# A fused encoder block: the first modulation sums move from VectorE to TensorE, projection weights are asked for one chunk earlier, and the routing pause and the gather are re-ordered

## The chip, the cores and the metric

The kernel runs on one core of a Trainium2 chip. The metric is the device time of one execution in microseconds (us). Five engines work beside each other: TensorE (PE in the profile, its weight loads PEld), VectorE (DVE), ScalarE (ACT), GpSimd (POOL) and SyncE (SP), which here only issues the large loads.

## The reference

One layer of a streaming encoder on 256 tokens of width 2048, all in float32:

```
mod = silu(c) @ ada_w + ada_b            # shift1, scale1, gate1, shift2, scale2, gate2
h = rmsnorm(x) * norm1_g * (1 + scale1) + shift1
u, v, q, k, v_b, gates = split(h @ w_in)             # 5 x 1024 and 2 x 2048 columns
y_a = spatial_gating(gelu(u), gelu(v)) @ w_branch_a  # 8 groups, 128 x 128 block-causal
y_b = band_attention(q, k, v_b) @ w_branch_b         # 16 heads, 64-frame chunks
x += gate1 * ((sigmoid(ga) * y_a + sigmoid(gb) * y_b) @ w_out)
h = rmsnorm(x) * norm2_g * (1 + scale2) + shift2
x += gate2 * moe(h)          # top 1 of 4 groups, then top 2 of 8 SwiGLU experts of width 512
return rmsnorm(x) * final_g
```

The weights of the 32 experts alone are 32 x 12.6 MB, those of the projections and of the modulation some 200 MB more; each is read once.

## The kernel before

**Buffers and queues.** Loads of 2 MB go through a ring of four buffers, `r0` to `r3` (`raws`, all named `r` in the profile); `load` (L111) and the modulation loads (L195) are issued from SP in the order in which the scheduler put them, and each waits until the last reader of its buffer is done. For the experts the ring grows to eight (`W`, `dC`, `dD`, `E` besides). A scheduler orders each engine's instructions, except where `pin` or `keep_in_program_order` holds them.

**Start.** `x` (two tiles of 128 tokens), the small vectors and the spatial weights `ws` are loaded. `ada_block(0, 4)` makes shift1 and scale1 for the first four of 16 column tiles of h: four loads of 2 MB from `ada_w`, and for each of 16 row tiles one DVE instruction (L205, L207) that adds `ada_w[row] * silu(c)[row]` into an accumulator `f`; then eight PE transposes (L217) and two reductions over the partitions (L220), and three small operations (L223 to L225) give `sh1`, `sg1`. Meanwhile ACT sums the squares of x (L251), POOL takes the root (L244), ACT scales x (L254), PE turns it (L259, 32 transposes) and ACT copies it to `hx` (L264). The turned `ws` become `wsT` (L269, L270). Then each column tile is scaled and shifted (L230), and split into a high part `hh` (tile `dC`, L233) and a low part `hl` (tile `dD`, L234).

**Projections.** `run_steps` multiplies h by a chunk of 512 rows x 1024 columns of weights in four k-steps. A step has 12 products of 128x512 (L292 to L294: high x high, low x high, high x low for two token tiles and two column halves); ACT casts the weights' high part (L318), DVE subtracts for the low part (L319), into two alternating buffers. The five `homes` (q, k, v and the two gMLP halves) are made in four blocks of four column tiles: the first block writes its sums with ACT (L351), the others add on DVE (L353). During a block, the `ada_block` of the next one runs in pieces between the steps; during the last block and all that follows the same is done for the other four modulation vectors (L435). Then come the gates beside attention and gMLP, the branches and the output projection, whose evacuation is L894 to L896.

**Routing and gather.** The last eight row tiles of gate2's second half (`LEFT = 2` loads) are not summed by DVE but by PE: `gate_steps` yields nine pairs of products, a first pair that sums the DVE accumulator over partitions with `ones` (L987), and eight with `R.scb` (L990). `fill` runs one pair after the output projection, `gate_some(6)` six while DVE works out the routing, and `gate_some(8)` the rest. With the positions known, DVE builds the 0/1 matrix `Gm` for the two token tiles (L1125, L1126), and PE multiplies `rsb` (the norm's factor) by it (L1168, result copied to `rsp`, L1173) and gathers h for all 512 token-expert pairs in four quarters `gather(q)` (L1183, 16 products each). DVE multiplies each result by `rsp` (L1196), ACT scales and shifts it (L1198), POOL copies the expert's window (L1292, L1294). The destination of quarters 0 and 1 (`x0`, `x1`) is also the buffer that their products read, so no result of a quarter is written before its 16 products are done. After quarter 1 the first half of expert 0 is multiplied (L1279), then quarters 2 and 3 follow, then its second half.

**Experts.** For each of 32 experts six loads of 2 MB (12.6 MB) come in through the ring of eight; `first_half` (L1279) and `second` (L1361) use them.

## Time and profile before

| what | value |
|---|---|
| median of 3 runs | 1690.38 us (1688.21 to 1690.66) |
| the profiled execution | 1689.86 us |
| its span in the trace | 1688.1 us |
| TensorE granted clock, mean | 0.972 |
| PE busy | 1538.8 us (91%) |
| moved by DMA | 625.25 MB, 370 GB/s over the span |

The span is what the trace covers; 1.8 us lie around it. "Granted clock" is the share of the full 2.4 GHz that TensorE was given, so 0.50 is 1.2 GHz. A busy PE may be a PE at half clock. DVE, ACT and PE wait for each other through semaphores; the trace shows for each instruction what released it.

### The profile page before, as it was taken

Reading aid. Unit: us, or ns where it says so; the run is one execution under the profiler, and the core shown is the slowest. Engines: PE = TensorE matmul, PEld = TensorE weight load, DVE = VectorE, ACT = ScalarE, POOL = GpSimd, SP = SyncE. Lnnn points to the kernel's source line nnn. Section 1 sums busy time; section 2 is a strip of 40 time slices with the busy share of each in tenths; the row PEclk is TensorE's granted clock in tenths of the full one; section 3 lists DMA queues with packets and bytes.
Section 4 is the critical chain, followed back from the end, with each engine's and each line's share of the span. In section 5 each row is a group of like instructions: output and inputs, shape, how many; then the busy total and the mean of one; then the engine's idle time right before and its main releaser. Section 6 shows DMA issues by size and latency. Waiting matters only on the chain.

```text
span 1688.1 us, 18245 instructions
## 1 busy us (share of the span) xinstructions
PE 1538.8 (91%) x6725; PEld 856.1 (51%) x6725; DVE 942.5 (56%) x1313; ACT 483.5 (29%) x785; POOL 126.3 (7%) x377
## 2 busy tenths in 40 slices
PE   2999999999999999999998989989899898898996
PEld 1777778777887776643333323334233333332432
DVE  5789999998778888734332333323333233332334
ACT  4554345675444345341110111101111011110112
POOL 1000000000000000011100101001011010100101
PEclk8999999999999999999999999999999999999998
DMA  9989897797988786899999999999999999999996
GB/s 359 343 315 341 336 341 299 296 343 273 351 313 315 305 312 244 343 384 418 416 418 417 416 418 416 417 418 416 418 416 418 418 416 418 416 417 417 416 419 245
DMA packets 135358, 625.25 MB, mean 370 GB/s; under 512 B 5720, under 2 KB 5840, under 8 KB 101856
## 3 DMA queue, kind: packets, MB, share of 16 engines
q1 hardware_dynamic: 132832, 614.49, 91.5%
q10 hardware_dynamic: 992, 5.28, 0.8%
q0 software_dynamic: 1440, 4.27, 0.8%
q8 instruction: 55, 0.90, 0.2%
q14 instruction: 39, 0.32, 0.0%
HBM read 621.91 MB, written 2.10 MB: 370 GB/s over the span
## 4 chain that ended last, share of the span: by engine, by line
PE 51%; DMA 42%; DVE 4%; issue 2%; ACT 1%; SPq 0%; POOL 0%; POOLq 0%; DVEq 0%; ACTq 0%
DMA r<-in_w_dram 22%; PE b L1279 12%; PE b L294 11%; PE b L292 11%; PE b L293 10%; DMA dC<-in_w_dram 9%; DMA E<-in_w_dram 8%; PE b L1361 3%; DMA r<-in_ada_w_dram 2%; DVE W L319 1%; DVE f L435 1%; PE b L1393 1%; DVE f L207 0%; PE b L1183 0%; PE b L593 0%
## 5 line engine op out<-in xcount | busy, mean ns | idle before, releaser
L1279 PE MATMUL b<-r,e 128*64 128x512 f32 x1024 | 376.3, 626 | 44.2 <-DMA r<-in_w_dram 43.6
L1395 DVE TENSOR_TENSOR dB<-dB,b 128x512 f32<-128x512 f32 x248 | 153.6, 681 | 317.4 <-PE b L1393 317.4
L318 ACT CAST W<-r 128x1024 fp32r<-128x1024 f32 (+1 forms) x224 | 220.8, 987 | 328.6 <-PE b L293 294.0
L319 DVE TENSOR_TENSOR W<-r,W 128x1024 fp32r<-128x1024 f32 (+1 forms) x224 | 255.8, 1147 | 64.5 <-ACT W L318 63.2
L292 PE MATMUL b<-W,dC 128*128 128x512 f32 x704 | 284.9, 405 | 5.3 <-ACT dC L233 3.7
L293 PE MATMUL b<-W,dD 128*128 128x512 f32 x704 | 280.0, 398 | 0.0
L294 PE MATMUL b<-W,dC 128*128 128x512 f32 x704 | 267.1, 398 | 2.3 <-DVE W L319 2.1
L1385 ACT CAST f<-f 64x512 fp32r<-64x512 f32 x124 | 76.4, 616 | 576.2 <-DVE dB L1395 414.2
L1279 PEld LDWEIGHTS b<-r,e 128*64 128x64 f32 x1024 | 116.7, 144 | 215.9 <-issue 144.1
L292 PEld LDWEIGHTS b<-W,dC 128*128 128x128 f32 x704 | 132.9, 189 | 40.8 <-ACT dC L233 4.1
L294 PEld LDWEIGHTS b<-W,dC 128*128 128x128 f32 x704 | 131.5, 188 | 38.9 <-DVE W L319 8.0
L435 DVE SCALAR_TENSOR_TENSOR f<-r,sc,f 128x1024 f32<-128x1024 f32 x115 | 147.2, 1281 | 4.5 <-DMA r<-in_ada_w_dram 3.7
L293 PEld LDWEIGHTS b<-W,dD 128*128 128x128 f32 x704 | 132.7, 189 | 30.4 <-issue 0.5
L1279 PE MATMUL b<-dC,e 128*64 128x512 f32 x256 | 120.0, 624 | 19.6 <-DMA dC<-in_w_dram 19.6
L1279 PE MATMUL b<-E,e 128*64 128x512 f32 x256 | 118.2, 616 | 19.4 <-DMA E<-in_w_dram 19.4
L1279 PE MATMUL b<-dD,e 128*64 128x512 f32 x256 | 127.2, 648 | 0.0
L1352 DVE TENSOR_TENSOR f2y<-f2y,b 128x256 f32<-128x256 f32 x31 | 13.1, 421 | 198.6 <-ACT f2y L1351 198.6
L1279 PE MATMUL b<-W,e 128*64 128x512 f32 x256 | 121.8, 625 | 0.0
L1361 PE MATMUL b<-r,f2y 128*64 128x512 f32 x496 | 111.3, 595 | 0.0
L1386 DVE TENSOR_TENSOR f<-f,f 64x512 fp32r<-64x512 f32 x124 | 85.1, 686 | 26.4 <-ACT f L1385 23.5
L1294 POOL COPY e<-a 128x64 f32 x256 | 68.7, 271 | 205.0 <-PE b L1279 191.1
L207 DVE SCALAR_TENSOR_TENSOR f<-r,sc,f 128x1024 f32<-128x1024 f32 x60 | 77.0, 1283 | 1.6 <-DMA r<-in_ada_w_dram 1.0
(321 smaller groups left out, 1475.5 us busy)
## 6 DMA issues: line engine op xcount, KB each, us to landing
r<-in_w_dram SPq DMA_DIRECT2D x93, 2048.0 KB, 28.2
r<-in_w_in_dram SPq DMA_DIRECT2D x36, 2048.0 KB, 8.4
r<-in_ada_w_dram SPq DMA_DIRECT2D x32, 2048.0 KB, 8.6
W<-in_w_dram SPq DMA_DIRECT2D x23, 2048.0 KB, 28.5
dC<-in_w_dram SPq DMA_DIRECT2D x23, 2048.0 KB
dD<-in_w_dram SPq DMA_DIRECT2D x23, 2048.0 KB, 28.2
E<-in_w_dram SPq DMA_DIRECT2D x23, 2048.0 KB, 28.1
r<-in_ada_w_dram SPq DMA_DIRECT2D x32, 1024.0 KB, 10.1
```

What stands on the lines that cost most here:

```text
L207: nc.vector.scalar_tensor_tensor(out=acc, in0=rw[:, jj], scalar=sc[:, j : j + 1], in1=acc, op0=ALU.mult, op1=ALU.add,)
L292: nc.tensor.matmul(o, a, wh[:, cs], start=(k == k0), stop=False)
L293: nc.tensor.matmul(o, b, wh[:, cs], start=False, stop=False)
L294: closed[0] = nc.tensor.matmul(o, a, wl[:, cs], start=False, stop=close)
L318: nc.scalar.copy(wh, src)
L319: nc.vector.tensor_sub(wl, src, wh.bitcast(F32))
L435: nc.vector.scalar_tensor_tensor(out=acc, in0=rw[:, jj, :], scalar=sc[:, j : j + 1], in1=acc, op0=ALU.mult, op1=ALU.add,)
L1279: nc.tensor.matmul(pab[a * CH : (a + 1) * CH, :], xe[:, 8 * half + j, :], w[:, j // JQ, j % JQ, :], start=(half == 0 and j == 0), stop=(ha ...
L1361: nc.tensor.matmul(po[a * CH : (a + 1) * CH, :], act[:, j, :], w[:, j, a * 512 : (a + 1) * 512], start=(j == 0), stop=(j == 3),)
L1385: pin(nc.scalar.copy(oh[r, a, :], og[r, b, :]))
L1386: pin(nc.vector.tensor_sub(oh[o, a, :], og[r, b, :], oh[r, a, :].bitcast(F32)))
L1395: pin(nc.vector.tensor_add(xa[:, t, d0 : d0 + 512], xa[:, t, d0 : d0 + 512], pr))
```

## The change

**Start.** The small vectors are loaded from SP (three loads, ahead of all others) and POOL (one) instead of ACT, and x first from ACT. A first Silu on a dummy value comes ahead of the real one. `ada_first` makes the first block's sums on PE: silu(c) is spread over 64 columns (`scb`), and each row tile of a load becomes two products of 64x512 into one bank, 32 in all; the two halves of the result are copied to `part`, turned by small products with `pick`, and shift and scale are finished for the first column tile alone and then for the other three. `hh` is then written in one step from `hx` by ACT, and `hl` from a DVE copy of the same value. x is scaled on DVE instead of ACT; the copies of the turned x alternate between ACT and DVE. Only the first quarter of the first weights chunk is asked for ahead of the fourth modulation load, the rest behind it. `ws` is loaded and turned (`turn_ws`) in the second block.

**Projections.** With `follow`, `run_steps` asks for the next home's weights ahead of its own modulation load. `ada_of` and `hurried` leave the pace of later blocks at one step per call, as it was.

**Routing and gather.** `left` adds one more row tile to the accumulator on DVE, so that there are eight pairs instead of nine, of which `gate_some(5)` runs five in the first pause. In quarter 0 the products of the first token tile come for all four banks, then the four products of the factors, then those of the second token tile.

```
     xt = [T([P, D], f"x{t}") for t in range(NT)]
-    rows = T([P, P], "a2")
-    nc.vector.memset(rows, 0.0)
-    r0 = 0
-    for src in (
-        c[0].rearrange("(j p) -> j p", p=P),
-        norm1_g[0].rearrange("(j p) -> j p", p=P),
-        ada_b[0, 0:D].rearrange("(j p) -> j p", p=P),
-        ada_b[0, D : 2 * D].rearrange("(j p) -> j p", p=P),
-        gmlp_b_s[0],
-    ):
-        nc.scalar.dma_start(out=rows[r0 : r0 + src.shape[0], :], in_=src)
-        r0 += src.shape[0]
     for t in range(NT):
         nc.scalar.dma_start(out=xt[t], in_=x[0, t * P : (t + 1) * P, :])
-    ws = [T([P, 4, P], "a0"), T([P, 4, P], "a1")]
-    for i in range(2):
-        nc.gpsimd.dma_start(out=ws[i], in_=gmlp_w_s[0, 4 * i : 4 * i + 4].rearrange("g t s -> t g s"))
+    r0 = 0
+    for src, queue in (
+        (c[0].rearrange("(j p) -> j p", p=P), nc.sync),
+        (norm1_g[0].rearrange("(j p) -> j p", p=P), nc.sync),
+        (ada_b[0, 0 : 2 * D].rearrange("(j p) -> j p", p=P), nc.sync),
+        (gmlp_b_s[0], nc.gpsimd),
+    ):
+        small = queue.dma_start(out=rows[r0 : r0 + src.shape[0], :], in_=src)
+        if queue is nc.sync:
+            small_last = small
+        r0 += src.shape[0]
+
+    nc.scalar.activation(mhalf[:, 1:2], mhalf[:, 0:1], AF.Silu)
+    nc.vector.memset(mhalf[:, 1:2], -0.5)
...
-    def ada_block(k0, n):
+    def ada_pieces(k0, n):
 
         w = n * P
-        acc = accs.sb([P, 2, w])
-        nj = 16 // n
+        nj = 4 if n > 2 or k0 == 0 else 8
         for j0 in range(0, ND, nj):
             rw = raws.sb([P, nj, 2, w])
             for m in range(2):
@@ -198,6 +200,58 @@
                         0, j0 * P : (j0 + nj) * P, m * D + k0 * P : m * D + k0 * P + w
                     ].rearrange("(j p) n -> p j n", p=P),
                 )
+            yield j0, nj, rw
+
+    def modulation(ks, sums):
+        nc.vector.tensor_add(sh1[:, ks], sums[:, 0, :], b_shift[:, ks])
+        nc.vector.tensor_add(sg1[:, ks], sums[:, 1, :], b_scale[:, ks])
+        nc.vector.scalar_tensor_tensor(
+            out=sg1[:, ks], in0=sg1[:, ks], scalar=1.0, in1=g1c[:, ks], op0=ALU.add, op1=ALU.mult
+        )
+
+    def ada_first(n):
+
+
+        w = n * P
+        scb = T([P, ND, CH], "f4")
+        nc.vector.tensor_copy(scb, sc.unsqueeze(2).to_broadcast([P, ND, CH]))
+        pick = T([P, 2], "pick")
+        nc.vector.tensor_copy(pick[:, 0:1], ident[:, 0:1])
+        nc.vector.tensor_copy(pick[:, 1:2], ident[:, CH : CH + 1])
+        pacc = bk.ps()
+        for j0, nj, rw in ada_pieces(0, n):
+            for jj in range(nj):
+                j = j0 + jj
+                for m in range(2):
+                    nc.tensor.matmul(
+                        pacc[m * CH : (m + 1) * CH, 0:w], scb[:, j, :], rw[:, jj, m, :],
+                        start=(j == 0), stop=(j == ND - 1),
+                    )
+            yield
+        part = T([P, w], "f0")
+        nc.scalar.copy(part[:, 0:P], pacc[:, 0:P])
+        nc.vector.tensor_copy(part[:, P:w], pacc[:, P:w])
+        for k0, k1 in ((0, 1), (1, n)):
+            tp = sk.ps()
+            for i in range(k0, k1):
+                nc.tensor.matmul(
+                    tp[:, 2 * (i - k0) : 2 * (i - k0) + 2], part[:, i * P : (i + 1) * P], pick,
+                    start=True, stop=True,
+                )
+            modulation(slice(k0, k1), tp[:, 0 : 2 * (k1 - k0)].rearrange("p (a b) -> p b a", b=2))
+            for j in range(k0, k1):
+                s, b = sg1[:, j : j + 1], sh1[:, j : j + 1]
+                nc.scalar.activation(hh[:, j, :], hx[:, j, :], AF.Identity, bias=b, scale=s)
+                full = scr[:, j * S : (j + 1) * S]
+                nc.vector.tensor_scalar(full, hx[:, j, :], s, b, op0=ALU.mult, op1=ALU.add)
+                nc.vector.tensor_sub(hl[:, j, :], full, hh[:, j, :].bitcast(F32))
+        yield
+
...
+    first = ada_first(BLOCKS[0])
+    with tc.issue_after(small_last.ins):
+        next(first)
     ss1 = T([P, NT], "ss1")
     scr = T([P, D], "e2")
-    for t in range(NT):
-        nc.scalar.activation(scr, xt[t], AF.Square, accum_out=ss1[:, t : t + 1])
+    with tc.issue_after(sc_made.ins):
+        for t in range(NT):
+            nc.scalar.activation(scr, xt[t], AF.Square, accum_out=ss1[:, t : t + 1])
     rs1 = inv_rms(ss1, "n1")
     for t in range(NT):
-        nc.scalar.activation(xt[t], xt[t], AF.Copy, scale=rs1[:, t : t + 1])
+        nc.vector.tensor_scalar(xt[t], xt[t], rs1[:, t : t + 1], None, op0=ALU.mult)
+    turned = Ring(["b2", "b3", "b4", "b5", "b6", "b0"])
     for j in range(0, ND, 2):
-        tp = bk.ps()
+        tp = turned.ps()
         for jj in range(2):
             for t in range(NT):
                 nc.tensor.transpose(
@@ -261,22 +335,43 @@
                     xt[t][:, (j + jj) * P : (j + jj + 1) * P],
                     ident,
                 )
-        nc.scalar.copy(hx[:, j : j + 2, :], tp.rearrange("p (a b) -> p a b", a=2))
+        tv = tp.rearrange("p (a b) -> p a b", a=2)
+        if j % 4 == 0:
+            nc.scalar.copy(hx[:, j : j + 2, :], tv)
+        else:
+            nc.vector.tensor_copy(hx[:, j : j + 2, :], tv)
+    with tc.issue_after(small_last.ins):
+        next(first)
+        next(first)
+
+        early = [raws.sb([P, 4, CW])]
+        nc.sync.dma_start(out=early[0][:, 0, :], in_=w_in[0, 0:P, 2 * GW : 2 * GW + CW])
+        for _ in first:
+            pass
     wsT = T([P, 8, P], "f3")
-    for i in range(2):
-        tp = bk.ps()
-        for g in range(4):
-            nc.tensor.transpose(tp[:, g * P : (g + 1) * P], ws[i][:, g, :], ident)
-        nc.scalar.copy(wsT[:, 4 * i : 4 * i + 4, :], tp.rearrange("p (a b) -> p a b", a=4))
-    nc.gpsimd.memset(wsT[CH:P, :, 0:CH], 0.0)
-    for _ in first:
-        pass
-
-
...
+            src = w[q * P : (q + m) * P, c0 : c0 + cw].rearrange("(j p) n -> p j n", p=P)
+            if early:
+                rw = early.pop()
+                tc.keep_in_program_order(nc.sync.dma_start(out=rw[:, 1:m, :], in_=src[:, 1:m, :]))
+            elif fetched:
+                rw = fetched.pop()
+            else:
+                rw = load([P, m, cw], src)
+            if follow is not None:
+
+                nk, nn, nc0 = follow
+                fetched.append(
+                    load([P, nn, cw], w[nk * P : (nk + nn) * P, nc0 : nc0 + cw].rearrange("(j p) n -> p j n", p=P))
+                )
...
+            follow = None
+            if h + 1 < len(homes):
+                follow = (k0, n, homes[h + 1][0])
+            elif not lastb:
+                follow = (k0 + n, BLOCKS[b + 1], homes[0][0])
...
+        if b == 0:
+            sides.append(turn_ws())
...
+            acc = accs[len(units) - 1]
+            j = ND - 4 * LEFT
+            nc.vector.scalar_tensor_tensor(
+                out=acc, in0=fetched[-LEFT][:, 0, :], scalar=sc[:, j : j + 1], in1=acc,
+                op0=ALU.mult, op1=ALU.add,
+            )
+            return fetched[-LEFT:], acc
...
-    gate_some(6)
+    gate_some(5)
...
+    def factors():
+        for t in range(NT):
+            for i in range(2):
+                pin(
+                    nc.tensor.matmul(
+                        prs, rsb[:, i, t, :], Gm[:, t, :], start=(t == 0 and i == 0), stop=(t == 1 and i == 1)
+                    )
+                )
+        nc.vector.tensor_copy(rsp, prs)
+
     rsp = T([P, PAIRS], "f2x")
-    nc.vector.tensor_copy(rsp, prs)
     Xg = []
 
     def gather(q):
-        banks = []
-        for j in range(JQ):
-            pg = bk.ps()
+        banks = [bk.ps() for _ in range(JQ)]
+
+        def products(j, t):
+            for i in range(2):
+                pin(
+                    nc.tensor.matmul(
+                        banks[j], x1p[q, t][i][:, j, :], Gm[:, t, :],
+                        start=(t == 0 and i == 0), stop=(t == 1 and i == 1),
+                    )
+                )
+
+
+        if q == 0:
             for t in range(NT):
-                for i in range(2):
-                    pin(
-                        nc.tensor.matmul(
-                            pg, x1p[q, t][i][:, j, :], Gm[:, t, :],
-                            start=(t == 0 and i == 0), stop=(t == 1 and i == 1),
-                        )
-                    )
-            banks.append(pg)
+                for j in range(JQ):
+                    products(j, t)
+                if t == 0:
+                    factors()
+        else:
+            for j in range(JQ):
+                for t in range(NT):
+                    products(j, t)```

The instruction order on PE at the start, from the program's first product to its first projection (names are tile_number; `a` holds the small vectors, then `ws`; `x` the tokens, `f` the accumulator, `r` the loads). Before:

```order
L169 MATMUL b_10_88<-ident_64,a_7_75 128x128
L259 MATMUL b_22_109<-ident_64,x_5_73 128x128
...
L259 MATMUL b_29_151<-ident_64,x_6_74 128x128
L269 MATMUL b_31_158<-ident_64,a_8_84 128x128 x4
L269 MATMUL b_32_164<-ident_64,a_9_85 128x128 x4
L217 MATMUL b_39_201<-ident_64,f_33_171 128x128 x4
L217 MATMUL b_40_207<-ident_64,f_33_171 128x128 x4
L292 MATMUL b_49_245<-W_63,dC_97 128x512
```

And now (`f_16_96` is `scb`, `f_36_206` is `part`):

```order
L172 MATMUL b_8_85<-ident_66,a_2_64 128x128
L226 MATMUL b_18_101<-r_19_102,f_16_96 64x512 x8
L226 MATMUL b_18_101<-r_32_171,f_16_96 64x512
L333 MATMUL b_24_123<-ident_66,x_6_75 128x128
...
L333 MATMUL b_31_165<-ident_66,x_7_76 128x128
L226 MATMUL b_18_101<-r_32_171,f_16_96 64x512 x7
L226 MATMUL b_18_101<-r_33_182,f_16_96 64x512 x8
L226 MATMUL b_18_101<-r_35_195,f_16_96 64x512 x8
L237 MATMUL b_37_209<-pick_98,f_36_206 128x2
L237 MATMUL b_38_217<-pick_98,f_36_206 128x2 x3
L387 MATMUL b_48_252<-W_63,dC_94 128x512
```

The 32 transposes of x stand between the first nine and the other 23 products of the sums, and the turning of `ws` is gone from here.

The order in which SP asks for the first loads. Before:

```order
L195 DMA r_34_172<-in_ada_w_dram 128x4x512 x2
L195 DMA r_35_179<-in_ada_w_dram 128x4x512 x2
L195 DMA r_36_186<-in_ada_w_dram 128x4x512 x2
L195 DMA r_37_193<-in_ada_w_dram 128x4x512 x2
L111 DMA r_46_233<-in_w_in_dram 128x4x1024
```

And now:

```order
L164 DMA a_2_64<-in_c_dram 16x128
L164 DMA a_2_64<-in_norm_g_dram 16x128
L164 DMA a_2_64<-in_ada_b_dram 32x128
L197 DMA r_19_102<-in_ada_w_dram 128x4x512 x2
L197 DMA r_32_171<-in_ada_w_dram 128x4x512 x2
L197 DMA r_33_182<-in_ada_w_dram 128x4x512 x2
L348 DMA r_34_193<-in_w_in_dram 128x1024
L197 DMA r_35_195<-in_ada_w_dram 128x4x512 x2
L405 DMA r_34_193<-in_w_in_dram 128x3x1024
```

The fourth modulation load now goes into the buffer of the first (`r0`) and stands behind a quarter of the weights.

PE from the routing pause to the end of quarter 0. Before (`f_442` is the DVE accumulator, `E` the routing's small tiles, `f_470` is `Gm`, `f2y_4712` is `rsb`, `x_430` quarter 0's tokens, `x_434` quarter 1's):

```order
L990 MATMUL b_457_4651<-r_454_4531,E_3826 64x512 x8
L990 MATMUL b_457_4651<-r_456_4649,E_3826 64x512 x4
L1101 MATMUL b_468_4739<-E_3826,ones_69 128x96 x2
...
L990 MATMUL b_457_4651<-r_456_4649,E_3826 64x512 x4
L1168 MATMUL b_476_4782<-f_470_4755,f2y_4712 128x512 x4
L1183 MATMUL b_480_4801<-f_470_4755,x_430_4298 128x512 x4
...
L1183 MATMUL b_485_4831<-f_470_4755,x_434_4317 128x512 x4
```

And now (`f_472` is `Gm`, `x_432` quarter 0's tokens):

```order
L1111 MATMUL b_459_4674<-r_456_4553,E_3848 64x512 x6
L1111 MATMUL b_459_4674<-r_458_4671,E_3848 64x512 x4
L1222 MATMUL b_470_4760<-E_3848,ones_71 128x96 x2
...
L1111 MATMUL b_459_4674<-r_458_4671,E_3848 64x512 x4
L1306 MATMUL b_482_4817<-f_472_4776,x_432_4320 128x512 x2
...
L1291 MATMUL b_478_4803<-f_472_4776,f2y_4733 128x512 x4
L1306 MATMUL b_482_4817<-f_472_4776,x_432_4320 128x512 x2
...
L1306 MATMUL b_487_4852<-f_472_4776,x_436_4339 128x512 x4
```

Ten products stand in the pause instead of twelve, and eight gather products stand ahead of the factors' four.

## Rows read from the trace of the kernel before

**Rows 1.** The page: GB/s of DMA in 40 equal slices of the span.

```profile
GB/s 359 343 315 341 336 341 299 296 343 273 351 313 315 305 312 244 343 384 418 416 418 417 416 418 416 417 418 416 418 416 418 418 416 418 416 417 417 416 419 245
```

**Rows 2.** Busy time by stretch: stretch, length, PE, PEld, DVE, ACT, POOL, clock, DMA share, GB/s.

```profile
45.00:100.00 55.00, 54.70 (x227) 43.30 (x228) 43.12 (x44) 30.29 (x44) 0.00 (x0) 0.95 0.93 350
...
160.00:220.00 60.00, 58.83 (x256) 46.80 (x255) 57.78 (x69) 26.26 (x33) 3.48 (x5) 1.00 0.85 318
...
640.00:700.00 60.00, 56.58 (x252) 40.60 (x251) 48.73 (x65) 31.28 (x55) 0.00 (x0) 1.00 0.67 250
...
836.00:1616.00 780.00, 697.56 (x2934) 267.18 (x2934) 261.34 (x442) 100.64 (x208) 76.64 (x259) 0.96 1.02 417
```

**Rows 3.** The chain in 0 to 60 us: start, length, work.

```profile
18.29 14.49 DMA r<-in_ada_w_dram
...
43.23 0.17 DVE sg L225
...
43.48 1.09 ACT dB L230 x2
...
44.92 0.80 PE b L292
...
49.59 0.43 PE b L293
...
52.16 0.23 PE b L294
```

**Rows 4.** The timeline, 0 to 30 us: start, length, instruction [idle before, releaser].

```profile
15.21 1.91 ACT L251 ACTIVATE e<-x 128x2048 f32<-128x2048 f32 x1 [3.56 <-DMA x<-in_x_dram]
16.66 0.76 DVE L205 TENSOR_SCALAR f<-r,sc 128x1024 f32<-128x1024 f32 x1 [6.53 <-DMA r<-in_ada_w_dram]
...
18.90 1.75 POOL L244 TENSOR_TENSOR rs_n<-ve_n,mhalf 128x2 f32<-128x2 f32 x1 [13.22 <-DVE ve_n L242]
20.68 3.90 ACT L254 ACTIVATE x<-x,rs_n 128x2048 f32<-128x2048 f32 x2 [3.47 <-POOL rs_n L244]
...
22.73 5.53 PE L259 MATMUL b<-ident,x 128*128 128x128 f32 x32 [12.93 <-ACT x L254]
...
28.10 1.04 PE L269 MATMUL b<-ident,a 128*128 128x128 f32 x8
```

**Rows 5.** Busy time by stretch (columns of rows 2): DMA rate, and the clock's fall.

```profile
20.00:30.00 10.00, 6.26 (x40) 5.62 (x40) 8.95 (x8) 8.28 (x11) 0.64 (x1) 1.00 1.05 386
...
32.00:33.00 1.00, 0.00 (x0) 0.00 (x0) 0.84 (x2) 0.00 (x0) 0.00 (x0) 0.95 1.05 412
33.00:34.00 1.00, 0.00 (x0) 0.00 (x0) 1.00 (x1) 0.00 (x0) 0.00 (x0) 0.50 1.02 406
```

**Rows 6.** Waits of PE between 50 and 700 us: total, times, longest.

```profile
PE b L294 <- DVE W L319: 4.3, 6, 1.7
PE b L292 <- ACT W L318: 1.6, 3, 1.1
```

**Rows 7.** The timeline of the routing pause and the gather.

```profile
703.29 5.37 PE L990 MATMUL b<-r,E 128*64 128x512 f32 x24
...
707.57 0.22 DVE L1093 TENSOR_TENSOR E<-E 128x64 f32<-128x64 f32 x1
...
708.59 0.69 PE L1101 MATMUL b<-E,ones 128*128 128x96 f32 x4
...
712.29 0.71 PE L1168 MATMUL b<-f,f2y 128*128 128x512 f32 x2 [0.53 <-DVE f L1126]
...
713.60 0.70 PE L1168 MATMUL b<-f,f2y 128*128 128x512 f32 x2 [0.60 <-DVE offc L1132]
...
714.14 7.63 PE L1183 MATMUL b<-f,x 128*128 128x512 f32 x32
```

**Rows 8.** SP's issues at the end of the gather.

```profile
744.32 0.55 SPq L111 DMA_DIRECT2D W<-in_w_dram  x1
```

**Rows 9.** Busy time (columns of rows 2) around that issue.

```profile
742.00:747.00 5.00, 3.66 (x22) 1.67 (x18) 0.00 (x0) 2.52 (x5) 3.42 (x18) 1.00 0.39 121
```

More of the change, by code (lines that the diff above doesn't have):

```diff
@@ L139, in flush @@
             tick()
+    rows = T([P, P], "a2")
+    nc.vector.memset(rows, 0.0)
     ident = T([P, P], "ident")
@@ L200, in ada_block @@
                 )
+            yield j0, nj, rw
[40 more added lines that the diff above has]
+        yield
+    def ada_block(k0, n):
+        w = n * P
+        acc = accs.sb([P, 2, w])
+        for j0, nj, rw in ada_pieces(k0, n):
             yield
@@ L222, in ada_block @@
             )
-        nc.vector.tensor_add(sh1[:, ks], sums[:, 0, :], b_shift[:, ks])
-        nc.vector.tensor_add(sg1[:, ks], sums[:, 1, :], b_scale[:, ks])
-        nc.vector.scalar_tensor_tensor(
-            out=sg1[:, ks], in0=sg1[:, ks], scalar=1.0, in1=g1c[:, ks], op0=ALU.add, op1=ALU.mult
-        )
+        modulation(ks, sums)
         yield
@@ L234, in ada_block, with ada_of, hurried @@
             nc.vector.tensor_sub(hl[:, j, :], hx[:, j, :], hh[:, j, :].bitcast(F32))
-            if j % 2 == 1:
+            if (j - k0) % 2 == 1 or j == k0 + n - 1:
                 yield
+    def ada_of(k0, n, calls):
+        parts = [n] if n <= 4 else [3, n - 3]
+        blocks, steps = [], 0
+        for m in parts:
+            blocks.append(ada_block(k0, m))
+            steps += (4 if m > 2 else 2) + ND + 1 + (m + 1) // 2
+            k0 += m
+        return hurried(itertools.chain(*blocks), max(1.0, steps / calls))
+    def hurried(g, rate):
+        due = 0.0
+        while True:
+            due += rate
+            while due >= 1.0:
+                due -= 1.0
+                if next(g, "end") == "end":
+                    return
+            yield
     def inv_rms(ss, name):
@@ L263, in hybrid_block, with turn_ws, run_steps @@
                 )
[L264 to L276 removed]
+        tv = tp.rearrange("p (a b) -> p a b", a=2)
[10 more added lines that the diff above has]
+            pass
+    wsT = T([P, 8, P], "f3")
+    def turn_ws():
+        ws = [T([P, 4, P], "a0"), T([P, 4, P], "a1")]
+        with tc.issue_after(casts[-1].ins):
+            for i in range(2):
+                nc.scalar.dma_start(out=ws[i], in_=gmlp_w_s[0, 4 * i : 4 * i + 4].rearrange("g t s -> t g s"))
+        yield
+        for i in range(2):
+            tp = sk.ps()
+            for g in range(4):
+                nc.tensor.transpose(tp[:, g * P : (g + 1) * P], ws[i][:, g, :], ident)
+            nc.scalar.copy(wsT[:, 4 * i : 4 * i + 4, :], tp.rearrange("p (a b) -> p a b", a=4))
+            yield
+        nc.gpsimd.memset(wsT[CH:P, :, 0:CH], 0.0)
+        yield
+    def run_steps(lh, ll, w, k0, n, c0, evac, with_ada=None, cw=CW, after=None, follow=None):
         nhf = cw // 512
         npc = 4096 // cw
+        npc = -(-n // -(-n // npc))
         pt = []
```

30 lines of the change are left out of this document (12 added, 18 removed).

## The prediction

> **What bounds the kernel now.** I read the page first: the GB/s row, which lies near 417 from the 19th slice to the last but one and lower and uneven before it [rows 1]. Then busy time by stretch, which says what each half waits for. From 836 to 1616 us the loads run at 417 GB/s without a break while PE is busy 697.6 of 780 us: the experts are bound by DMA [rows 2]. From 45 to 700 us it is PE: it idles 0.3 us in 45 to 100, 1.17 in 160 to 220, 3.42 in 640 to 700 [rows 2]. So the kernel is a stretch paced by PE, then a stream of bytes whose rate nothing here changes. A load is issued when a reader frees its buffer, so the stream starts when PE gets there. A microsecond saved on PE's way to 700 us is a microsecond at the end, as long as DVE and the loads keep pace with PE; one saved between 700 and 744 us counts only while DMA stands idle. The chain of waits then shows the way to the first projection: the modulation loads, DVE's sums, transposes, a first product at 44.92 us [rows 3]. The timeline of that stretch gives what the pieces cost [rows 4], a finer table by stretch the clock [rows 5], and the timelines of the gather and of SP the second place [rows 7, 8].
>
> **The start.** The last of the four modulation loads lands at 32.78 us (18.29 + 14.49) [rows 3]; then come four DVE sums, eight transposes, reductions, modulation, scaling and split, and PE starts at 44.92, 12.1 us after the landing. It starts at half clock: products follow each other every 0.43 us, and later every 0.23 [rows 3]. The clock had dropped to 0.50 in the 33rd microsecond, when PE had been idle since the end of the transposes at 29.14 (28.10 + 1.04) [rows 4, 5]. With 12 products of 0.427 us the first k-step ends at 50.05.
>
> Now the same with the change. *Landing.* Ahead of the fourth load's end stand x (2.1 MB), four loads (8.4) and a quarter of the weights (0.5); before it was `ws` (0.5) in the place of that quarter. The bytes are equal, and DMA was busy throughout at 386 GB/s [rows 5]. I take 32.0 us, a little early for the small packets of `ws` that are gone; the bounds are 31.3 and 33.5. The fourth load needs `r0`, whose products end by about 17 us, when some 3 MB still queue, so that wait is covered. *Products.* A pair of 64x512 products has a row: 24 records, that is 12 products, in 5.30 us or so, 0.44 us each [rows 7]. A load is eight of them, 3.5 us, against 5.4 us for its bytes (2.1 MB at 386 GB/s). PE must have the rest done when the last load lands. x's second half has its squares done at 17.2 us now [rows 4]; asked for first, it should land some 3 us earlier, near 12.3, so squares end near 14.4, POOL's root (1.75) near 16.6, and DVE's scaling of the two tiles, 1.5 us each (twice the 0.76 of 128x1024), at 18.2 and 19.7; ACT took until 24.6 [rows 4]. The transposes stand behind the first product of the second load, which lands near 18.5 to 19; they take 5.5 us [rows 4], to 24.6; then 15 products, 6.6 us, to 31.2. That is just before 32.0, so the last eight start on landing and end at 35.5. *Tail.* Copy to `part`, small products, three DVE operations of 0.17, one ACT instruction of 0.55 (half of 1.09) [rows 3] and the handoffs: 2.0 us is my estimate (1.5 to 3.0). First projection at 37.5, and, at full clock, 12 x 0.233 = 2.8 us later, at 40.3, the first k-step is done. DVE has the low part of the second column tile ready at about the same time, so I see no new wait there. **40.3 - 50.05 = -9.75 us.**
>
> The clock in this sum rests on a pattern: PE is never idle for over 2 us from 13 us on, and before, an idle stretch of 13 us ahead of the transposes (12.93 us, to 22.73 [rows 4]) still found the full clock. The Trainium skill (TensorE: Matmul & The Clock Gate, Part 4: PE-mode transpose) says that the full clock does not engage for transposes, since they do not count as busy in the same way. Here the 32 transposes ran in 5.53 us with the clock at 1.00 in their stretch [rows 4, 5], but nothing shows whether they hold it up. By that rule the clock could fall in the middle of the new chain; what this would cost is a rival below.
>
> **What is moved behind the start.** The eight transposes of `ws` took 1.04 us beside DVE's sums, where PE had nothing to do [rows 4]. Now they stand in the second block, where PE sets the pace: **+1.04 us.** Their load is asked for about four k-steps before PE needs it, so it is covered; the two copies are on ACT, which is busy 26 of 60 us there [rows 2].
>
> **Weights a chunk ahead.** I cost it at nothing. Each load still needs the buffer of the load four earlier in the ring, so a home's weights are asked for when those of two homes earlier have been split, as before: about 11 us before they are needed, of which the transfer takes 5.4. In the second and third block SP now often issues a modulation load ahead of weights, but its buffer is free earlier too. The possible gain is small: waits for a split are 4.3 + 1.6 us in all of 50 to 700 [rows 6].
>
> **The pause and the gather.** In the pause PE ends its twelve products only as L1101 starts at 708.59, though DVE had its operand at 707.79 (707.57 + 0.22) [rows 7]. With ten products PE is free at 707.7: the chain is 0.78 us earlier. Next, PE waits between the two pairs of factor products, from about 12.8 to 13.60, and quarter 0 is 16 products of 0.234 behind them [rows 7]. Now eight gather products fill that time, since they need only the first tile's matrix; of the 36 products from 712.29 to the end of quarter 1 at 721.77, none waits any more: 36 x 0.234 = 8.4 us instead of 9.5. In all quarter 1 ends some 1.65 to 1.85 us earlier, and with it expert 0's first half, the other quarters and the second half, at whose end SP asks for the next load, at 744.32 [rows 8]. DMA had run dry by then: in 742 to 747 us it moved 121 GB/s, so 5 x (1 - 121/417) = 3.55 us were lost [rows 9]. An issue 1.65 us earlier fills that much: **-1.65 us.** Were the stream not dry, this part would be worth nothing. The added DVE sum (1.28 us) falls into the last output chunk, where DVE, busy 48.7 of the 60 us in 640 to 700 [rows 2], has time to spare and the split is a step ahead: nothing, at most half of it, 0.6.
>
> **Sum.** -9.75 + 1.04 - 1.65 = -10.4 us against the profiled 1689.86: 1679.5. That execution lies 0.5 us below the median of 1690.38, so I predict **1680.0 us**.
>
> **Rivals.**
> *A: the clock falls among the transposes and comes back.* For it speaks the rule above. Coming back took about 5 us of dense products (44.92 to 50). Six of the 15 products then cost 0.87 instead of 0.44: the last eight start at about 33.5, end at 37: 1681.5; two such dips 1684.
> *B: half clock throughout, from the first sum to the end of the first k-step.* Loads' products take 7 us, transposes about 8.6: PE is at 29.5 after them, at 42.4 after 15 products, 49.3 after the last, 51.3 with the tail, and 56.4 after the first k-step: 6.4 us later than before, so 1690.4 + 6.4 + 1.04 - 1.65 = **1696, slower**. It decides when PE still has over some 14 us of sums left as the last load lands; against it speaks the full clock until 32.9 us [rows 5]. If only what follows the transposes stays at half, it is about 1691.
> *C: the middle eats part of it.* DVE is busy 57.8 of 60 us in 160 to 220 [rows 2]. If weights land behind a modulation load asked for at the same moment, they come 5.4 + 5.4 + 2 us after the issue, 1.4 us late; in four homes that is 5.6 us: 1685.6.
> *D: x or the small vectors come late*, so transposes start near 22 instead of 19: the sums end 2 to 3 us later, 1682.5.
> *E: weights a chunk ahead does work*, and the 5.9 us of split waits [rows 6] mostly go: 1675.
>
> **Chances.** The forecast, 1677.5 to 1682.5: 0.66. A 0.10, D 0.06, C 0.08, E 0.03, about 1691 0.03, B 0.04. The low end takes the best tail, landing and gather (-1.5 - 0.7 - 0.2, and 1 us of split waits): 1676.5; the high end reaches A, D and C: 1686.5. What a measurement of this kernel can tell from no change is about 0.2%, 3.4 us. Faster by more than that (below 1687.0): 0.88; within: 0.07; slower: 0.05.
>
> **What the profile will show.** Right: the first L387 near 37.5 us and PE's clock 1.00 from 13 us on; L226 in groups of eight of 3.5 us; stretches of 45 to 700 as full as before but some 9 us earlier; and DMA's hole before the third load of `W` down to 1.9 us. Wrong: a clock of 0.50 before 40 us; PE waiting for DVE's split in the second and third block more than 5 us; quarter 1 no earlier against the end of the output projection; or a stream of experts that does not run at 417.

## The result

The changed kernel takes **1705.45 us** (median of 4 runs, 1704.63 to 1706.60), the kernel before 1690.25: a ratio of 1.0094 (95% interval 1.0081 to 1.0106), 15.2 us slower. Forecast were 1680.0 us and a range of 1676.5 to 1686.5. The profiled execution took 1706.04, its span is 1704.2. From the first expert load into `W` to the end of the span it takes 989.2 us, where it took 990.4 before; the time is lost ahead of the experts. The start comes first. The timeline of PE in the changed kernel, 9 to 41 us (start, length, instruction, idle time before it), answers to [rows 3, 4]:

```profile
12.31 1.94 PE L226 MATMUL b<-r,f 128*64 128x512 f32 x2 [2.67 <-DMA r<-in_ada_w_dram]
14.93 5.91 PE L226 MATMUL b<-r,f 128*64 128x512 f32 x16 [0.68 <-DMA r<-in_ada_w_dram]
20.77 3.71 PE L333 MATMUL b<-ident,x 128*128 128x128 f32 x32
24.41 7.09 PE L226 MATMUL b<-r,f 128*64 128x512 f32 x32
32.46 3.65 PE L226 MATMUL b<-r,f 128*64 128x512 f32 x14 [0.96 <-DMA r<-in_ada_w_dram]
36.46 0.38 PE L237 MATMUL b<-pick,f 128*128 128x2 f32 x2 [0.36 <-ACT f L232]
37.28 0.80 PE L237 MATMUL b<-pick,f 128*128 128x2 f32 x6 [0.43 <-DVE sg L207]
38.07 0.73 PE L387 MATMUL b<-W,dC 128*128 128x512 f32 x2
39.18 0.50 PE L388 MATMUL b<-W,dD 128*128 128x512 f32 x1 [0.38 <-DVE dD L247]
...
40.82 0.63 PE L388 MATMUL b<-W,dD 128*128 128x512 f32 x1
```

The start went nearly as forecast: the last modulation load lands at 32.4, the sums end at 36.11 (32.46 + 3.65), the first projection comes at 38.07. Busy time by stretch shows the clock (the third column from the end): it is full among the transposes and is 0.50 in 40 to 43 us.

```profile
20.00:25.00 5.00, 5.00 (x40) 3.78 (x38) 2.48 (x4) 2.35 (x4) 0.00 (x0) 1.00 1.05 390
...
40.00:43.00 3.00, 3.00 (x9) 2.32 (x8) 2.43 (x5) 1.00 (x3) 0.00 (x0) 0.50 1.03 383
...
100.00:160.00 60.00, 49.59 (x209) 39.05 (x209) 47.99 (x54) 22.35 (x28) 0.52 (x1) 0.94 0.78 284
160.00:220.00 60.00, 55.27 (x238) 43.43 (x237) 55.82 (x65) 23.28 (x28) 1.53 (x2) 1.00 0.82 302
```

Where the lead goes is in the last two rows: PE has 49.59 us of work in 100 to 160 and 55.27 in 160 to 220. The kernel before had 58.83 in the second of these stretches [rows 2], and in the first:

```profile
100.00:160.00 60.00, 58.94 (x258) 46.88 (x257) 55.86 (x62) 26.77 (x34) 0.00 (x0) 1.00 0.88 327
```

The waits of PE in the changed kernel (total, times, longest), in 100 to 160 the first two, in 160 to 220 the third, in 220 to 280 the fourth:

```profile
PE b L362 <- DMA a<-in_gmlp_w_s_dram: 6.6, 1, 6.6
PE b L389 <- DVE W L427: 3.0, 3, 1.7
...
PE b L389 <- DVE W L427: 4.7, 4, 2.3
...
PE b L389 <- DVE W L427: 3.7, 2, 2.3
```

The end of each home tells it most plainly. The table takes the moment at which the first of a home's four evacuations (L351 and L353 before, L459 and L461 now) starts, and gives for each kernel how much later than before it is (minus: earlier). The columns to the right belong to the experiments below. Each column is read from one profiled execution; that of run 1 (1693.39 us) was 2.5 us slower than the median of its runs.

| home's end | before, us | changed | weights as before | and `ws` early | casts first at three ends | chunk ahead, on the kernel before |
|---|---|---|---|---|---|---|
| block 1, 1st | 56.64 | -6.95 | -7.03 | -7.00 | -6.86 | 0.37 |
| 2nd | 67.84 | -6.95 | -5.15 | -5.12 | -6.10 | 0.38 |
| 3rd | 79.05 | -6.97 | -3.27 | -3.25 | -5.61 | 0.38 |
| 4th | 90.27 | -6.51 | -1.41 | -1.39 | -5.45 | 0.35 |
| 5th | 103.61 | -6.78 | -0.67 | -0.64 | -4.72 | -0.86 |
| block 2, 1st | 114.34 | 8.08 | 2.13 | 0.23 | -3.85 | 4.15 |
| block 3, 2nd | 185.55 | 14.29 | 2.18 | 0.28 | -3.78 | 10.54 |
| block 4, 5th | 279.24 | 17.27 | 2.59 | 0.34 | -3.98 | 11.28 |

The lead of 7 us is whole until the first block's end and gone at once: 14.9 us are lost between the fifth home and the next, 9 more until the fourth block's end.

### The profile page after: what moved, and what is told of

Same layout as the page of the kernel before. It is cut to its first block, busy times and chain, and to the rows that moved or that the text cites. A ratio compares the mean times of both kernels' runs of the same rounds, so it can differ in the third digit from the quotient of the medians.

```text
span 1704.2 us, 18349 instructions
## 1 busy us (share of the span) xinstructions
PE 1559.1 (91%) x6785; PEld 865.0 (51%) x6785; DVE 930.8 (55%) x1314; ACT 477.0 (28%) x776; POOL 126.3 (7%) x376
## 4 chain that ended last, share of the span: by engine, by line
PE 44%; DMA 42%; issue 6%; DVE 5%; ACT 1%; POOL 0%; SPq 0%; POOLq 0%; DVEq 0%; ACTq 0%
DMA r<-in_w_dram 22%; PE b L1413 12%; DMA dC<-in_w_dram 9%; PE b L389 9%; PE b L387 8%; DMA E<-in_w_dram 8%; PE b L388 8%; PE b L1495 3%; DMA r<-in_ada_w_dram 2%; DVE W L427 2%; DVE f L261 1%; PE b L1527 1%; PE b L226 1%; DMA a<-in_gmlp_w_s_dram 1%; PE b L1306 0%
## 5 line engine op out<-in xcount | busy, mean ns | idle before, releaser
L427 DVE TENSOR_TENSOR W<-r,W 128x1024 fp32r<-128x1024 f32 (+1 forms) x224 | 255.1, 1144 | 81.7 <-ACT W L426 80.5
L387 PE MATMUL b<-W,dC 128*128 128x512 f32 x704 | 283.7, 404 | 3.1 <-ACT W L426 3.1
L388 PE MATMUL b<-W,dD 128*128 128x512 f32 x704 | 280.2, 398 | 0.4 <-DVE dD L247 0.4
L389 PE MATMUL b<-W,dC 128*128 128x512 f32 x704 | 267.8, 400 | 12.2 <-DVE W L427 12.1
L1413 PEld LDWEIGHTS b<-r,e 128*64 128x64 f32 x1024 | 120.3, 146 | 212.3 <-issue 139.0
L389 PEld LDWEIGHTS b<-W,dC 128*128 128x128 f32 x704 | 131.1, 188 | 50.9 <-DVE W L427 20.2
L387 PEld LDWEIGHTS b<-W,dC 128*128 128x128 f32 x704 | 132.9, 189 | 38.9 <-ACT W L426 5.5
L549 DVE SCALAR_TENSOR_TENSOR f<-r,sc,f 128x1024 f32<-128x1024 f32 x115 | 147.0, 1279 | 3.9 <-DMA r<-in_ada_w_dram 3.2
L388 PEld LDWEIGHTS b<-W,dD 128*128 128x128 f32 x704 | 132.8, 189 | 31.7 <-issue 0.8
L1413 PE MATMUL b<-E,e 128*64 128x512 f32 x256 | 124.4, 643 | 22.9 <-DMA E<-in_w_dram 22.9
L1413 PE MATMUL b<-dC,e 128*64 128x512 f32 x256 | 116.2, 608 | 17.8 <-DMA dC<-in_w_dram 17.8
L1413 PE MATMUL b<-dD,e 128*64 128x512 f32 x256 | 123.3, 630 | 0.4 <-DMA dD<-in_w_dram 0.4
L1413 PE MATMUL b<-W,e 128*64 128x512 f32 x256 | 117.4, 608 | 0.3 <-DMA W<-in_w_dram 0.3
L1413 PEld LDWEIGHTS b<-E,e 128*64 128x64 f32 x256 | 36.4, 147 | 80.8 <-issue 48.6
```

The lines of the kernel that those rows point to most:

```text
L387: nc.tensor.matmul(o, a, wh[:, cs], start=(k == k0), stop=False)
L388: nc.tensor.matmul(o, b, wh[:, cs], start=False, stop=False)
L389: closed[0] = nc.tensor.matmul(o, a, wl[:, cs], start=False, stop=close)
L427: nc.vector.tensor_sub(wl, src, wh.bitcast(F32))
L549: nc.vector.scalar_tensor_tensor(out=acc, in0=rw[:, jj, :], scalar=sc[:, j : j + 1], in1=acc, op0=ALU.mult, op1=ALU.add,)
L1413: nc.tensor.matmul(pab[a * CH : (a + 1) * CH, :], xe[:, 8 * half + j, :], w[:, j // JQ, j % JQ, :], start=(half == 0 and j == 0), stop=(ha ...
```

## The experiments

**The theories.** *Q, the queue's order:* SP asks in order. A home's weights wait for the buffer that the home before gives back; now the modulation load of a home stands behind the weights of the next one, and so behind a wait that ends about a home, 11.2 us, later. DVE's sums then end with the block and not a home ahead. *S:* the late `ws` load and what follows it start it all. *M:* the early start itself asks more of DMA and DVE than they have. What Q looks like in the changed kernel, on SP and on DVE:

```profile
59.47 0.37 SPq L111 DMA_DIRECT2D r<-in_w_in_dram  x1
60.66 1.08 SPq L197 DMA_DIRECT2D r<-in_ada_w_dram  x2
71.52 0.37 SPq L111 DMA_DIRECT2D r<-in_w_in_dram  x1
74.03 0.92 SPq L197 DMA_DIRECT2D r<-in_ada_w_dram  x2
...
95.32 3.92 DVE L261 SCALAR_TENSOR_TENSOR f<-r,sc,f 128x1024 f32<-128x1024 f32 x3
100.05 0.69 DVE L274 TENSOR_REDUCE sums<-b 128x4 f32<-128x512 f32 x1 [0.81 <-PE b L271]
```

The last modulation load for the second block goes out at 74.03; DVE ends its sums at 99.24 (95.32 + 3.92), when PE has ended the block's last product at 98.9. What SP waited for ahead of the loads at 71.52 and 74.03:

```profile
SPq L111 <- DVE W L427: 9.7, 1, 9.7
SPq L197 <- DVE f L261: 2.1, 1, 2.1
```

The weights load waits 9.7 us for a buffer, and the modulation load behind it is not issued meanwhile; then it waits 2.1 us for its own buffer.

**1. Weights as before.** `with_ada=nxt, follow=follow` becomes `with_ada=nxt`; all else as changed.

> The changed kernel, but each home's weights are asked for in their own home again (no weights load ahead of the modulation load on SP); all else stays. Theory Q (queue order: a weights load that waits for its buffer holds back the modulation load behind it by one home of about 11.2 us, so DVE's sums end at the block's end instead of a home earlier): the sums for the second block end some 10 us before the first block's end, PE is fuller in 100 to 280 us, and about two thirds of the 24.8 us that are lost between the first and the 80th weight cast come back; what stays is the wait for ws: 1686 to 1692 us. Theory S (the late ws load and the half clock behind it start it all, and DVE never catches up): 1702 to 1706 us. Theory M (the early start itself asks more of DMA and DVE in the middle than they give): 1698 us or more, with PE waiting for the splits as in the changed kernel.

Measured: 1690.87 us, ratio to before 1.0007 (0.9997 to 1.0016): 14.6 us back. The same rows of this run:

```profile
61.30 0.37 SPq L111 DMA_DIRECT2D r<-in_w_in_dram  x1
65.14 0.92 SPq L197 DMA_DIRECT2D r<-in_ada_w_dram  x2
...
87.35 3.92 DVE L261 SCALAR_TENSOR_TENSOR f<-r,sc,f 128x1024 f32<-128x1024 f32 x3
92.08 0.69 DVE L274 TENSOR_REDUCE sums<-b 128x4 f32<-128x512 f32 x1 [0.81 <-PE b L271]
```

The load goes out 8.9 us earlier and the sums end at 91.27, 11.7 us ahead of the fifth home's end (103.61 - 0.67). Q holds; S falls, and the total is not M's either (1698 or more). The Trainium skill (DMA: Bandwidth & Descriptors, Anatomy of one DMA — SWDGE (gpsimd) path) says that a transfer's wait for a semaphore happens on the sequencer that issues it, before dispatch. The rows agree (the section is on transfers that GpSimd issues, these are SP's): in the changed kernel the modulation loads at 60.66 and 74.03 are issued only once the weights' have been, at 59.47 and 71.52.

**2. `ws` asked for early.** The two loads move into a generator that runs in the first block:

```
+    def load_ws():
+        with tc.issue_after(casts[-1].ins):
+            ...
+    sides.append(load_ws())
```

> The changed kernel, but the two loads of ws are issued in the first block behind the second weight cast (about 38 us) instead of at its end (99.01 us); the eight transposes stay where they are. Theory Q: the wait of 6.6 us for ws goes, but PE then waits for the first scaled column tile until about 104.7 instead of starting it at 108.8, so 4 us come back and perhaps 1.5 of the half clock: 1699 to 1702 us. Theory S: most of the loss goes, 1682 to 1688 us. Theory M: 1699 to 1702, as Q.

Measured: 1702.01 us, ratio 1.0074 (1.0057 to 1.0091): 3.4 us back, a little less than the 4 of Q. The wait for `ws` is gone; the other cost of the late sums is not. Not all of the 3.4 us need be the load's: in the profiled execution the clock stayed full in 40 to 43 us, and the first home ended 8.58 us earlier than before instead of 6.95.

**3. Chunk ahead on the kernel before.** `follow` and `fetched` alone are added to it.

> The kernel before, with one thing of the change: each home's weights are asked for a home ahead, in front of the modulation load. Theory Q: the modulation loads go out a home later, the sums end at the block's end in every block, and this alone costs 10 to 18 us: 1700 to 1708 us. Theory S and theory M: no late ws and no early start, so within 2 us of 1690.3; what the prediction had said of this edit is the same, nothing or up to 5.9 us faster.

Measured: 1702.68 us, ratio 1.0075 (1.0058 to 1.0092): 12.5 us slower, with no early start and no late `ws`. DVE's last sum of the first block's `ada_block` ends at 99.65 in it, and PE waits for the splits in 100 to 280 us:

```profile
98.37 1.28 DVE L209 SCALAR_TENSOR_TENSOR f<-r,sc,f 128x1024 f32<-128x1024 f32 x1
...
PE b L296 <- DVE W L327: 10.1, 6, 3.7
```

**4. Modulation load ahead.** In the changed kernel two statements change places: `next(with_ada, None)` stands ahead of the load for `follow`.

> The changed kernel with two statements swapped: the modulation load of a home is issued ahead of the next home's weights load, so that weights are still asked for a home ahead but no modulation load stands behind them. Theory Q (the modulation loads lose a home on SP's queue): the sums end about a home before the first block's end again, the 24.8 us shrink as in the run with the weights as before, 1688 to 1693 us. Rival P (asking for weights ahead fills the ring of four buffers, whichever stands first, so DVE's sums and the splits stay late): 1700 us or more.

Measured: 1690.51 us, ratio 1.0001 (0.9991 to 1.0010). The two statements are all that differs from the changed kernel, and they set the order on SP: so it is the place on the queue. Rival P is not tested apart from that: in the first two blocks the loads are issued in the very order of run 1, so that on SP the weights are not ahead any more.

**5. Both: weights as before, `ws` early.**

> The changed kernel with both: weights asked for in their own home, ws loaded in the first block. Theories Q and S: the gain of the start at the first block's end (6.95 us by the casts) and that of the gather (1.2 us at the end) stay, less 1.04 us for the transposes of ws in the second block: 1682 to 1685 us. Theory M: the middle eats the start's gain, 1688 to 1691 us.

Measured: 1689.66 us, ratio 1.0002 (0.9993 to 1.0012). Against run 1 the 1.2 us for `ws` are about what its noise allows. This is a miss for Q: the lead of 7.00 us at the first home's end is 0.64 at the fifth's, some 1.9 less at each end of a home. M, or something else, was still to be found.

**6. Pause and gather alone**, on the kernel before.

> The kernel before with the last part of the change alone: the added DVE sum, eight pairs of gate products with five in the pause, and the first tokens first in the gather's first quarter. By the prediction's term 1.65 us faster, 1688.5 us; by the changed kernel's trace (late by 17.3 us at the last weight cast, 15.6 at the 11th expert load, 16.1 to 16.5 among the experts) some 1 us of it is left at the end, 1689.0 us. Rival G (the stream has no hole that could be filled once the loads behind are counted): 1690.1 us.

Measured: 1688.69 us, ratio 0.9995 (0.9985 to 1.0004). The median moves by 1.4 us; the interval takes in nothing as well. The traces agree with a gain: SP issues the load of [rows 8] at 742.81 instead of 744.32, and the expert loads behind it land 1.5 us earlier in the median.

**7. Chunk ahead in the first block alone**, `ws` early (`if b == 0 and h + 1 < len(homes)`).

> The changed kernel with ws loaded in the first block and the weights asked for a home ahead in the first block alone, not across its end nor in the others. Theory Q: inside the first block PE keeps 7 to 8 us, as in the changed kernel, and pays about 6 us at its end for the sums that come too late; the other blocks lose nothing more: 1687 to 1691 us. Rival P: the late sums of the first block carry over into the next ones, 1695 us or more. If the sums came in time, 1682 us.

Measured: 1693.26 us, ratio 1.0022 (1.0012 to 1.0031). Between the two expectations. ACT's weight casts run 8.4 us ahead of before in the first block, 1.7 behind at the second home's cast of the next one, 4.3 behind in the fourth: the late sums cost more than the lead. (The clock stayed full in 40 to 43 us here too.)

**8. Fewer bytes**, on run 5: for `k0 == 4` only `rw[:, 0]` is loaded and used.

> The version with the weights as before and ws loaded in the first block (1689.66 us), but of the modulation weights for the second block only one row tile of four is loaded and used four times, which leaves out 6.3 MB of loads during the first block; the instructions on PE, DVE and ACT are the same. Theory D (with an earlier start the first block is bound by its loads, 400 GB/s from 50 to 80 us, and so eats the start's gain): PE's waits for weights of 5.3 us between 36 and 100 us go, the weight casts stay 8 to 10 us earlier than before up to the first block's end, and the total falls to 1680 to 1684 us. Theory M2 (DVE or the order of its sums eats the gain): no more than 2 us faster than 1689.66.

Measured: 1682.14 us, ratio 0.9963 (0.9949 to 0.9977): the lead stays, 6.1 to 7.5 us at the ends of the first block's homes. It looks like proof of D, but the scheduler plans with the loads and wrote another order for ACT as well; at the second home's end a cast now stands ahead of the copies, which it does not in run 5 (below):

```profile
60.12 1.05 ACT L430 CAST W<-r 128x1024 fp32r<-128x1024 f32 x1 [1.75 <-PE b L392]
61.08 1.96 ACT L463 COPY e<-b 128x512 f32<-128x512 f32 x3
```

So the run says that the lead can be kept, not why.

**9. A spare buffer.** On run 5, the second home's weights go to the two x buffers.

> The version with the weights as before and ws loaded in the first block (1689.66 us), and the second home's weights of the first block loaded into the two x buffers, which are free from the last transpose (24.4 us) until the fourth home writes its results there; the ring of four buffers is then one load ahead in the first block. All bytes are loaded. Theory D (the first block is bound by its loads, and the hole in them at 45 to 50 us, where 214 GB/s were moved because all four buffers were taken, makes it worse): weights for the third home land near 58 us instead of 61.4, those for the fourth near 68 instead of 72.3, both before PE needs them; PE's waits for weights of 5.3 us go, and the total is 1682 to 1685 us. If the bytes alone decide, whatever the buffers: 1687 to 1690 us. Theory M2 (DVE's order): no change, 1689 to 1690 us.

Measured: 1688.72 us, ratio 0.9994 (0.9985 to 1.0003): not D's total, but that for "the bytes alone decide". DMA moved 372 GB/s in 45 to 50 us instead of 214, and nearly nothing came of it: the third home's weights landed at 60.7 us, the fourth's at 71.2. What run 5's waits of 1.6 us wait for is in its own trace. PE's waits in 36 to 100 us, and ACT at the second home's end:

```profile
PE b L390 <- ACT W L429: 5.3, 4, 1.6
...
62.72 2.68 ACT L462 COPY e<-b 128x512 f32<-128x512 f32 x4 [2.68 <-PE b L392]
65.30 2.00 ACT L429 CAST W<-r 128x1024 fp32r<-128x1024 f32 x2
```

The weights had landed at 61.4; the cast that PE waits for stands behind four copies, and these behind PE's last product of the home. In the kernel before the cast comes first at this end:

```profile
66.89 1.05 ACT L318 CAST W<-r 128x1024 fp32r<-128x1024 f32 x1 [1.75 <-PE b L293]
67.84 1.97 ACT L351 COPY e<-b 128x512 f32<-128x512 f32 x3
```

*Theory O:* the order of ACT costs 1.6 us and more at each end. That the scheduler chose it because it took the loads to come late is a guess. The Trainium skill (Perfetto Trace Analysis, Tensor Engine Instruction) says that ACT takes its instructions strictly in order; these rows agree.

**10. Casts first.** `tc.keep_in_program_order` on ACT's casts and copies of the first block, on run 5.

> The version with the weights as before and ws loaded in the first block (1689.66 us), and in the first block ACT's casts and evacuation copies held in the order of the program: a home's first cast ahead of the four copies of the home before (in 1689.66 us they stand behind them, and PE idles 1.6 us for that cast at each of four ends of homes). Theory O (this order of ACT, made for loads that come late, eats the start's gain): the four waits of 5.3 us and what follows them go, PE ends the first block 5 to 7 us earlier, total 1682 to 1686 us. Theory D (the weights themselves land too late: third home's at 61.4, fourth's at 72.3 us): the cast then stands waiting for its load, PE's waits stay within 1 us of 5.3, total 1688.5 to 1690.5 us.

Measured: 1693.76 us, ratio 1.0028 (1.0019 to 1.0037). A miss that decides nothing: the hold also put the very first cast behind the writing of `hh` (first cast at 40.6 instead of 27.0 us) and delayed the block's end. With the spare buffer besides it was 1694.38, where O had 1682 to 1686 and D about 1688.7: a miss too. **11. At the four inner ends alone:**

> The version with the weights as before and ws loaded in the first block (1689.66 us), with the hold on ACT's order at the four ends of homes inside the first block alone: the next home's first cast ahead of the four copies; the start and the block's end are left to the scheduler, since the wider hold put the first cast of all behind the writing of hh (first product 4 us later) and delayed the block's end. Theory O: first weight cast at 27 us as in 1689.66 us, no wait of 1.6 us at the ends of homes, PE ends the block 5 to 7 us earlier than with 1689.66 us, total 1682 to 1685 us. Theory D (loads): the held cast waits for its weights, which landed at 61.4 and 72.3 us; PE's waits stay near 5 us and the total within 1.5 us of 1689.66.

Measured: 1690.64 us, ratio 1.0002 (0.9993 to 1.0011). The total is the one of D, within 1.5 us of 1689.66, and a miss for O. But the lead was 6.66, 6.33 and 6.21 us at the first three ends, as O says, and then the copies of the fourth stood behind the scaling of the next block's columns. With the spare buffer it was 1692.06, where 1682 to 1685 (O) or within 1.5 of 1688.72 (D) had been expected. **12. At the first three ends alone**, where the cast and the copies change places on ACT and a product or so on PE; up to 280 us, SP and DVE keep the order of run 5:

```
-                    casts.append(nc.scalar.copy(wh, src))
+                    casts.append(hold[0](nc.scalar.copy(wh, src)) if first_cast else nc.scalar.copy(wh, src))
```

> The same hold at the first three ends of homes only, where ACT's order differs from 1689.66 us in nothing but the first cast standing ahead of the four copies. With the hold at four ends PE kept its lead (6.66 us at the first end, 6.21 at the third, against 7.00 and 3.25 without) and lost it at the fourth, where the copies came to stand behind the scaling of the next block's columns (PE waited for the banks), so the total did not move. Theory O: a lead of 6 us at the third end, one wait of 1.6 to 1.9 us at the fourth, about 4 us at the block's end and in the blocks behind, total 1685 to 1687 us. If the weights bind (third home's landed at 60.5, fourth's at 71.8 us): the lead is lost to 3 us and less by the block's end, total 1688 to 1690 us.

Measured: **1685.88 us**, ratio **0.9980 (0.9971 to 0.9990)**: 0.2% faster than the kernel before, and inside O's range. ACT at the second end, and PE's waits for the casts in 36 to 100 us:

```profile
60.78 1.05 ACT L430 CAST W<-r 128x1024 fp32r<-128x1024 f32 x1 [1.86 <-DMA r<-in_w_in_dram]
61.74 2.56 ACT L463 COPY e<-b 128x512 f32<-128x512 f32 x4
...
PE b L391 <- ACT W L430: 0.5, 1, 0.5
```

The cast now waits for its load (1.86 us) and is still in time for PE. So the order ate most of the lead, and the loads stand close behind it: the lead at the fifth home's end is 4.72 us, not 7.00. O holds. That the loads (D) are the next limit is argued from this wait; no run shows it, and what takes the other 2.3 us of the lead was not parted further.

## Why the prediction was wrong, point by point

**The step that failed** is "Weights a chunk ahead. I cost it at nothing". Its reason, that SP often issues a modulation load ahead of weights "but its buffer is free earlier too", looked at the buffers and at one direction of the exchange. What changed is that the modulation load stands behind the next home's weights, whose buffer comes free a home later. Runs 1 and 3 price it from both sides: 14.6 us with the change around it, 12.5 alone, where 0 was written and up to 5.9 faster was rival E. One of the signs of being wrong that the prediction names came with it: PE waited for DVE's split 3.0 + 4.7 = 7.7 us in the second and third block, where more than 5 was to count. Rival C had the queue's order as its mechanism, but the wrong way round (weights behind modulation) and at 5.6 us.

**The start** was to give 9.75 us. Its pieces came within 0.6 us (32.4 for 32.0; 36.1 for 35.5; 38.07 for 37.5), but the first k-step ended near 43.0, not 40.3: 7.0 us at the first home's end. Some 1.4 of these 2.7 us are the clock, 0.50 from 40 to 43 us: in runs 2 and 7, where it stayed full, the step ended at 41.6 and 41.7, and the lead at the first home's end was 8.58 and 8.43. The rest is the start of the projection, 0.6 us late, and small waits in the step, of which the profile shows one of 0.38 us for DVE's split of h. That the sum then carried this to the end of the kernel was the second fault, hidden behind the first: with the weights as before it is worn down to 0.64 at the block's end (run 5); with all loads in place and ACT's order mended, 4.72 are left there (run 12). "As long as DVE and the loads keep pace" was said and not worked out.

**The clock.** PE was to be at full clock from 13 us on; through the start it was, but for the 3 us from 40 on, which come behind a stretch (36.1 to 39.5) with three gaps of 0.36 to 0.43 us and a handful of products. These gaps alone do not explain the fall: runs 2 and 7 have them too, and run 2 shows in 40 to 43 us

```profile
40.00:43.00 3.00, 3.00 (x15) 2.40 (x14) 2.71 (x6) 1.80 (x3) 0.00 (x0) 1.00 1.03 383
```

Rival A put the fall among the transposes, by the rule of the Trainium skill (TensorE: Matmul & The Clock Gate, Part 4: PE-mode transpose); here 32 transposes ran in 3.71 us at a clock of 1.00, among products. Rival B did not come.

**`turn_ws`** was to cost 1.04 us with its load "asked for about four k-steps before PE needs it". It was issued at 99.01, at the block's end, took 8.95 us beside a modulation load issued at 95.43 and a weights load issued at 99.27, and PE waited 6.64 us. Of these at most 3.4 us mattered in the changed kernel (run 2), since the first scaled column tile was not there until about 104.7 either; 1.2 with the weights as before. The turning itself was sized about right: in runs 5 and 12 the lead shrinks by 0.87 us between the last home of the first block and the next, where the transposes stand.

**Pause and gather** held: L1222 comes at 725.23, and the 36 products from 728.81 to 737.35 take 8.5 us instead of 9.5. Counted from the output projection's end, where the kernel is 17.3 us late, L1222 comes 0.66 us earlier than L1101 did (forecast 0.78), and quarter 1 ends 1.72 us earlier (1.65 to 1.85). The rows of the changed kernel that answer to [rows 8, 9]:

```profile
759.90 0.55 SPq L111 DMA_DIRECT2D W<-in_w_dram  x1
...
757.00:762.00 5.00, 4.24 (x24) 1.83 (x20) 0.00 (x0) 1.95 (x4) 4.04 (x20) 1.00 0.80 297
```

The hole shrank from 3.55 to 1.4 us (5 x (1 - 297/417)), or to 1.6 in 757.58 to 762.58, the stretch that lies about the issue as that of [rows 9] does (283 GB/s); 1.9 was forecast. The kernel was 17.3 us late ahead of the pause (first load into `W` issued at 715.05 instead of 697.75) and 16.1 by the spans: 1.2 of the 1.65 are there at the end, 1.4 in run 6.

**The sum** by the runs: 1689.66 - 1690.13 for what is left in run 5, + 1.2 for the late `ws` (run 1), + 14.6 for the queue: 15.3. It meets the 15.2 measured by construction, since each term is the step from one run to the next, and proves nothing. What speaks for the size of the queue's term is that it comes out alike in other company: 12.5 on the kernel before (run 3), 12.35 with `ws` asked for early (1702.01 - 1689.66).

## What to carry to other kernels

A load that is asked for earlier on an in-order queue delays everything behind it until its buffer is free: price a prefetch by what stands behind it, not by its own wait. When an early stage is sped up, follow its lead from end to end of the next units before writing it down to the end of the kernel; an order of instructions that is fixed ahead of time can give it back although the data come in time. And where an experiment takes bytes away, look whether the order of the engines changed with it.

## What the runs showed of the hardware

The clock was 1.00 through the start although PE had idled 9.19 us before its first product and 2.67 after it; it fell to 0.50 at about 40 us, in a stretch in which PE had been busy most of the time since 12.3 us, behind the three short gaps. In the profiled executions of runs 2, 7 and 11 the same stretch (36 to 45 us) ran at 1.00, with the same gaps and the same busy time of PE in 36 to 40 us (2.83 or 2.84 us, as in the changed kernel). So the gaps do not bring the fall by themselves. Each kernel has one profiled execution, so whether the fall goes with the kernel or differs from one execution to the next is not shown.
